# Where a two-layer decoder kernel reads the second copy of feature tile 0, and where it builds its bias table

## The chip, the cores and the metric

The kernel runs on one core of one Trainium2 chip. The metric is device time in microseconds (us), the median of several runs. The profile is one execution on the same kind of chip, recorded instruction by instruction.

## The reference

A batch of one sequence of 256 tokens with 1024 features passes through two layers, all in float32. Layer 0 has a gated short convolution and a gated feed-forward net (ConvGLU, 2816 hidden features). Layer 1 has block attention with 16 heads over keys and values computed once, and a second ConvGLU. Cut to what matters here:

```python
def rms_norm(x, g):
    y = x * lax.rsqrt(jnp.mean(x * x, axis=-1, keepdims=True) + EPS)
    return y * g
...
x = x + short_conv_mixer(rms_norm(x, a_norm), a_w_in, a_conv, a_w_out)   # layer 0
x = x + conv_glu_ffn(rms_norm(x, f_norm[0]), ...)
k, v, k_mean = shared_kv(x, kv_norm, w_k, w_v)
x = x + moba_attention(rms_norm(x, b_norm), w_q, w_o, k, v, k_mean, rel_bias)   # layer 1
x = x + conv_glu_ffn(rms_norm(x, f_norm[1]), ...)
return rms_norm(x, final_norm)
```

With 256 tokens there is a single attention block, so attention is plain causal softmax attention with a bias that depends on the distance between two tokens (`rel_bias`, 32 buckets by 16 heads).

## The kernel before, in words

**Products in three parts.** Activations are kept transposed, features on the 128 partitions and the 256 tokens along a row, as eight feature tiles k = 0 to 7. Every float32 weight block and every activation is split into a high and a low part, and a product is three TensorE matmuls (`mm3`, L163 to L166): high weights by high activations (`xh`, L164), high weights by low activations (`xl`, L165), low weights by high activations (L166). Nearly all of them load 128x128 weights and stream 256 columns. `up_step` (L168) runs a 1 MB unit of weights (two halves, 8 tiles, 3 matmuls: 48) or a 512 KB unit (24) into one PSUM bank; `down_step` (L194) is 24 matmuls into four banks. ScalarE makes the high parts (L86), VectorE the low ones (L92), SyncE (SP) issues the loads (L80), three units ahead.

**Norms come late.** The products run on activations that are scaled by the gain alone, and each result is multiplied by the root of its token afterwards. So each of the four stages with a norm (mixer, FFN of layer 0, V, FFN of layer 1) has two small products in true float32 in the middle of its first units, and both interrupt the stream of split matmuls. The first, in `rstd_cols` (L323), adds up the squares: "the sums of squares". VectorE then takes the root (L327, L308 to L313) and builds a diagonal matrix `dg` (L331). The second, in `rstd_rows` (L337), multiplies `ones` by `dg`: "the spread of the roots" over the partitions. The code places each by hand between two parts of an `up_step`, with the feature tiles left and right of it written out.

**The second copy.** `Rows` (L246) lays out `xh` and `xl`. The eight tiles start at element 48 + 256 of a row; a second place for tile 0, `again`, starts at element 32. With 4 bytes each, the eight tiles begin at byte 1216 = 9 x 128 + 64 of their row and `again` at byte 128 = 1 x 128: seen in steps of 128 bytes, the copy lies half a step off from the tiles. In the mixer and in layer 0's FFN, `tile_0_again` (L262) copies tile 0 there, and `up_step(..., again=True)` reads the copy in place of tile 0. In layer 1's FFN (`moved=True`) tile 0 lives only in that second place, so each of that FFN's 22 units reads it there, whatever `again` says.

In before, the copy is read in these places of layer 0: right behind the sums of squares of the mixer (L427) and of the FFN (L525); right behind the spread of the roots of the mixer (L435: tiles 0, 3 to 7, with 1 and 2 ahead of it) and of the FFN (L529, unit 2); and in unit 4 of the mixer (L459), right behind the bias table.

**The bias table.** `bias_table` (L346) is a third float32 product, `rb` by a one-hot matrix `hot`, 33 by 16 by 384. ScalarE copies it out of PSUM (L350) and stores it to DRAM (`ext_d`, L351), from where SP loads a piece per head pair (`bias_pair`, L353), the first one after V's unit 2. In before the product stands in the mixer, between its second `down_step` and unit 4 (L456), in the `misc` bank; `rb` and `hot` are loaded at the start (L153, L155).

Of the kernel before, what the change touches and what calls it, by code (L numbers as in the profile page):

```python
# [11 lines left out]
F32 = mybir.dt.float32  # L12
# [30 lines left out]
def yoco_kernel(ctx: ExitStack, tc: tile.TileContext, t: dict, out: bass.AP):  # L43
    nc = tc.nc
# [5 lines left out]
    tmp = ctx.enter_context(tc.tile_pool(name="tmp", bufs=2))  # L50
    dram = ctx.enter_context(tc.tile_pool(name="dram", bufs=1, space=bass.MemoryType.DRAM))
    psum = ctx.enter_context(tc.tile_pool(name="psum", bufs=1, space=bass.MemoryType.PSUM))
# [61 lines left out]
    MC = [Unit(t["w_mc"][j], BIG) for j in range(KT)]  # L114
# [35 lines left out]
        u.load()  # L150
    nc.sync.dma_start(pk[:, P_FCW:], t["pk"][:, P_FCW:])
    rb = tmp.tile([33, NH], F32, name="rb", bufs=1)
    nc.sync.dma_start(rb, t["rb"])  # L153
    hot = tmp.tile([33, 384], F32, name="hot", tag="sc", bufs=3)
    nc.sync.dma_start(hot, t["hot"])  # L155
    ident = const.tile([128, 128], F32, name="ident")
    make_identity(nc, ident)

# [9 lines left out]
    def up_step(u, o, xh, xl, m, ks=range(KT), first=0, again=False):  # L168

        assert u.lo is not None  # L170
        wh, wl = u.v(u.hi, m), u.v(u.lo, m)
        for k in ks:
            h, lw = (xh.again, xl.again) if again and k == 0 else (xh[:, k, :], xl[:, k, :])
            for i in range(m):
                mm3(o[:, i, :], wh[:, k, i, :], wl[:, k, i, :], h, lw,
                    start=(k == first and i == 0), stop=(k == KT - 1))
        u.used = ks[-1] == KT - 1
# [52 lines left out]
    def up_bank():  # L230
        return psum.tile([128, 2, S], F32, name="up", bufs=3)
# [111 lines left out]

    ext_d = dram.tile([NH, 384], F32, name="ext_d")

    def bias_table():  # L346
        ps = psum.tile([128, 512], F32, name="misc", bufs=1)
        PE.matmul(ps[:NH, :384], rb, hot, start=True, stop=True)
        e = tmp.tile([NH, 384], F32, name="ext", tag="pr", bufs=4)
        A.activation(e, ps[:NH, :384], AF.Copy)  # L350
        nc.scalar.dma_start(ext_d, e)  # L351
# [17 lines left out]
    mc, mb, z = {}, {}, {}  # L369
# [58 lines left out]
    mb[1] = acc_bank()  # L428
    up_step(MB[1], mb[1], xh, xl, 1)
    mc[2] = up_bank()  # L430
    up_step(MC[2], mc[2], xh, xl, 2, (1, 2), first=1)
    rr = rstd_rows(dg)
    A.activation(rr[:, 1, :], rr[:, 0, :], AF.Square)
    lo("S")
    up_step(MC[2], mc[2], xh, xl, 2, (0, 3, 4, 5, 6, 7), first=1, again=True)  # L435
    mb[2] = psum.tile([128, 512], F32, name="misc", bufs=1).rearrange("p (a s) -> p a s", s=S)
    up_step(MB[2], mb[2], xh, xl, 1)
    for i in range(2):
# [13 lines left out]
    for i in range(2):  # L452
        down_step(MO[i], acc, z[i], first=(i == 0))
        hi("S")
        lo("S")
    bias_table()  # L456
    for j in range(4, KT):
        mc[j] = up_bank()
        up_step(MC[j], mc[j], xh, xl, 2, again=(j == 4))  # L459
        o = mixer_a(j, "S")  # L460
        mb[j] = up_bank()
        up_step(MB[j], mb[j], xh, xl, 1)
        hi("S")
        mixer_b(j, o, "B" if j < KT - 1 else "S")
        if j < KT - 1:
            lo("S")
        if j == KT - 3:
            lo("B")
        down_step(MO[j - 2], acc, z[j - 2])
        hi("S")  # L470
        if j == KT - 1:
            lo("S")
# [8 lines left out]
    def ffn(layer, xh, xl, sq, bank=down_bank, between=None):  # L481
        ub, hd, low = {}, {}, {}
        up, dn = UP[layer], DN[layer]

        def conv(j, last=False):
            c0 = 2 * FJ * layer + j
            cw = [[par(P_FCW, 3 * (c0 + half * FJ) + n) for n in range(3)] for half in range(2)]
            u = tmp.tile([128, 2, S], F32, name="u", bufs=2)
            V.tensor_mul(u, ub[j], rr[:, 0:1, :].to_broadcast([128, 2, S]))  # L489
            if j:  # L490
                low[j - 1]()
            if not last:
                lo("B")
            o = tmp.tile([128, 2, S], F32, name="cv", bufs=2)
            for half in range(2):
                A.activation(o[:, half, :], u[:, half, :], AF.Identity, scale=cw[half][2],  # L496
                             bias=par(P_FCB, c0 + half * FJ))
            hi("B")
            for back in (1, 2):
                for half in range(2):  # L500
                    tap(o[:, half, :], u[:, half, :], cw[half][2 - back], back)
            return o

        def gate(j, o, last=False):
            sl = tmp.tile([128, S], F32, name="sl", tag="sc", bufs=3)
            hi("S")
            A.activation(sl, o[:, 0, :], AF.Silu)
            lo("S", 0, 1 + last)
            hid = tmp.tile([128, S], F32, name="hid", tag="pr", bufs=4)
            V.tensor_mul(hid, sl, o[:, 1, :])  # L510
            hd[j], zh, low[j] = split_act(hid, S)
            zh()
            if last:
                lo("S", 1, 2)
                low[j]()

        acc = None
        for i in range(FJ):
            ub[i] = up_bank()
            if i == 1:  # L520
                up_step(up[1], ub[1], xh, xl, 2, range(1, 4), first=1)
                _, dg = rstd_cols(sq)
                lo("S")
                A.activation(first, ones[:, 0:1], AF.Silu)
                up_step(up[1], ub[1], xh, xl, 2, (0, 4, 5, 6, 7), first=1, again=True)  # L525
                rr = rstd_rows(dg)
                gate(0, conv(0))
            else:
                up_step(up[i], ub[i], xh, xl, 2, again=(i == 2))  # L529
            last = i == FJ - 1  # L530
            if i:
                o = conv(i, last)
                if not last:
                    gate(i, o)
            if i == 0 and between:
                between()
            if i >= LAG:
                if i == LAG:
                    acc = [acc_bank() for _ in range(4)]
                down_step(dn[i - LAG], acc, hd[i - LAG], first=(i == LAG), bank=bank)  # L540
            if last:
                gate(i, o, True)
            elif i == FJ - 2:
                hi("S")
                lo("S")
            if i == 0:
                hi("B")
        if bank is token_bank:
            token_last(dn[FJ - 3:], acc, [hd[j] for j in range(FJ - 3, FJ)])
        else:  # L550
            down_step(dn[FJ - 3], acc, hd[FJ - 3])
            down_last(dn[FJ - 2:], acc, [hd[FJ - 2], hd[FJ - 1]])
        return acc

    acc = ffn(0, xh, xl, sq)


    xvh, xvl, sq = boundary(acc, xT, P_KVN, rev)
    xqh, xql = parts_tiles()
    vh = wpool.tile([128, 2, D], F32R, name="vh", tag="hiB2")  # L560
# [155 lines left out]
    for kind, n in heads:  # L716
        if kind == "v":
            vb[n] = acc_bank() if n < 3 else up_bank()
            if n == 1:
                v_step(1, range(0, 4))  # L720
                ycol, dg = rstd_cols(sq)
                v_step(1, range(4, 8))
                oh = shifted(act, "oh", "oh", KT, bufs=1)
            elif n == 2:
                v_step(2, range(0, 2))
                rr = rstd_rows(dg, (-0.125, 1.0), (rev, same))
                v_step(2, range(2, 8))
                bias[0] = bias_pair(0)
            else:
                v_step(n)  # L730
# [181 lines left out]
```

## Time and profile before

| | us |
|---|---|
| median of 3 runs | 594.75 (594.44 to 594.77) |
| the profiled execution's own time | 594.58 |
| its span in the trace | 592.5 |
| TensorE matmul (PE) busy | 583.1, 98%, 4745 records |
| weight load (PEld) busy | 568.1, 96% |
| VectorE (DVE) busy | 461.0, 78% |
| ScalarE (ACT) busy | 359.7, 61% |
| GpSimd (POOL) busy | 3.6, 1% |

The profiled execution took 2.1 us more than its span. A matmul's record starts when the matmul starts and ends when its last result is out, so the records overlap: 0.28 us long, they start every 0.11 to 0.12 us. How fast the stream runs is therefore read from the starts, over many matmuls, not from the busy share. In the rows of the timeline the columns are start, duration, engine, line, operation, tiles out<-in, shape and count.

### The profile page before, as it was taken

To read this page: it belongs to the slowest core of one execution; us is meant where nothing else is said; L and a number is where in the kernel's file an instruction comes from. 1 tells how busy PE (TensorE), PEld (TensorE's weight loads), DVE (VectorE), ACT (ScalarE), POOL (GpSimd) and SP (SyncE) were. 2 spreads that over 40 slices of the span, in tenths; PEclk is the share of its full clock that TensorE was granted. 3 is DMA by queue.
4 is the path that set the end of the run, shared out by engine and by line. 5 is a ranking of instruction groups with operands and counts; after the bars stand their busy time and mean duration, and the time that the engine had idled before them with its cause. 6 is when DMAs were issued, how large, how long until landed. Compare 5 with 4: busy or idle time off the path is not lost.

```text
span 592.5 us, 11536 instructions
## 1 busy us (share of the span) xinstructions
PE 583.1 (98%) x4745; PEld 568.1 (96%) x4745; DVE 461.0 (78%) x781; ACT 359.7 (61%) x570; POOL 3.6 (1%) x15
## 2 busy tenths in 40 slices
PE   8999999999999999999999999999999999999995
PEld 8999999999999999999999999999999999999994
DVE  5998769888877787778887898747997877778765
ACT  7765337566654565455767999738675655556434
POOL 0000000000000000000000000000000000000001
PEclk9999999999999999999999999999999999999998
DMA  8975583546445544554355564442646445553211
GB/s 294 401 282 180 177 285 109 176 144 248 159 168 210 212 156 170 210 208 149 108 189 221 197 210 157 170 142 106 241 152 238 177 165 202 213 203 117 72 37 71
DMA packets 24236, 108.51 MB, mean 183 GB/s; under 512 B 2759, under 2 KB 5496, under 8 KB 16248
## 3 DMA queue, kind: packets, MB, share of 16 engines
q1 hardware_dynamic: 23864, 107.46, 50.4%
q8 instruction: 37, 0.61, 0.4%
q10 hardware_dynamic: 320, 0.32, 0.2%
q14 instruction: 15, 0.12, 0.1%
HBM read 106.70 MB, written 1.07 MB: 182 GB/s over the span
## 4 chain that ended last, share of the span: by engine, by line
PE 97%; DMA 1%; ACT 1%; DVE 0%; issue 0%; SPq 0%; POOLq 0%; POOL 0%; DVEq 0%; ACTq 0%
PE up L164 20%; PE up L165 20%; PE up L166 20%; PE acc L164 7%; PE acc L165 7%; PE acc L166 7%; PE acc L192 3%; PE acc L191 3%; PE acc L190 3%; PE acc L619 1%; PE acc L575 1%; PE acc L578 1%; PE acc L577 1%; DMA xres<-xT 1%; PE up L578 0%; PE up L575 0%
## 5 line engine op out<-in xcount | busy, mean ns | idle before, releaser
L164 PE MATMUL up<-xh,hiB 128*128 128x256 f32 x944 | 265.6, 281 | 0.7 <-ACT hiB L86 0.6
L166 PE MATMUL up<-xh,loB 128*128 128x256 f32 x944 | 263.9, 280 | 0.5 <-DVE loB L92 0.5
L165 PE MATMUL up<-xl,hiB 128*128 128x256 f32 x944 | 264.0, 280 | 0.0
L164 PEld LDWEIGHTS up<-xh,hiB 128*128 128x128 f32 x944 | 179.5, 190 | 2.7 <-ACT hiB L86 1.1
L166 PEld LDWEIGHTS up<-xh,loB 128*128 128x128 f32 x944 | 177.4, 188 | 0.9 <-DVE loB L92 0.9
L165 PEld LDWEIGHTS up<-xl,hiB 128*128 128x128 f32 x944 | 177.3, 188 | 0.8
L92 DVE TENSOR_TENSOR loB<-rawB,hiB 128x2048 fp32r<-128x2048 f32 (+2 forms) x75 | 147.5, 1972 | 3.6 <-ACT hiB L86 3.5
L86 ACT ACTIVATE hiB<-rawB 128x2048 fp32r<-128x2048 f32 (+1 forms) x73 | 123.4, 1694 | 19.4 <-issue 6.2
L496 ACT ACTIVATE cv<-u,pk 128x256 f32<-128x256 f32 x88 | 48.2, 595 | 79.2 <-DVE u L489 79.2
L92 DVE TENSOR_TENSOR loS<-rawS,hiS 128x1024 fp32r<-128x1024 f32 (+2 forms) x73 | 83.6, 1146 | 14.4 <-ACT hiS L86 14.0
L366 DVE SCALAR_TENSOR_TENSOR cv<-u,pk,cv 128x255 f32<-128x255 f32 x192 | 81.2, 477 | 2.6 <-ACT cv L496 1.7
L489 DVE TENSOR_TENSOR u<-up,rr 128x512 f32<-128x512 f32 x44 | 30.3, 690 | 64.9 <-PE up L166 63.6
L86 ACT ACTIVATE hiS<-rawS 128x1024 fp32r<-128x1024 f32 (+1 forms) x71 | 71.6, 1010 | 11.8 <-PE acc L165 7.6
L166 PE MATMUL acc<-sh,loS 128*128 128x256 f32 x240 | 67.5, 281 | 0.0
L165 PE MATMUL acc<-sl,hiS 128*128 128x256 f32 x240 | 67.5, 281 | 0.0
L164 PE MATMUL acc<-sh,hiS 128*128 128x256 f32 x240 | 67.5, 281 | 0.0
L363 ACT ACTIVATE sh<-hid 128x256 fp32r<-128x256 f32 x52 | 21.7, 417 | 59.7 <-DVE hid L510 54.9
L164 PEld LDWEIGHTS acc<-sh,hiS 128*128 128x128 f32 x240 | 46.1, 192 | 0.0
L166 PEld LDWEIGHTS acc<-sh,loS 128*128 128x128 f32 x240 | 45.1, 188 | 0.0
L165 PEld LDWEIGHTS acc<-sl,hiS 128*128 128x128 f32 x240 | 45.1, 188 | 0.0
L192 PE MATMUL acc<-hiS,sl 128*128 128x512 f32 (+1 forms) x89 | 34.9, 392 | 0.0
L191 PE MATMUL acc<-loS,sh 128*128 128x512 f32 (+1 forms) x89 | 34.7, 390 | 0.0
(157 smaller groups left out, 757.2 us busy)
## 6 DMA issues: line engine op xcount, KB each, us to landing
rawB<-w_up SPq DMA_DIRECT2D x44, 1024.0 KB, 4.8
rawS<-w_dn SPq DMA_DIRECT2D x44, 512.0 KB, 3.4
rawB<-w_qk SPq DMA_DIRECT2D x8, 1024.0 KB, 4.8
rawB<-w_mc SPq DMA_DIRECT2D x6, 1024.0 KB, 8.8
rawS<-w_mo SPq DMA_DIRECT2D x8, 512.0 KB, 4.1
rawB<-w_v SPq DMA_DIRECT2D x4, 1024.0 KB, 4.7
rawS<-w_o SPq DMA_DIRECT2D x8, 512.0 KB, 3.4
rawS<-w_mb SPq DMA_DIRECT2D x7, 512.0 KB, 5.6
```

The lines of the kernel that those rows point to most:

```text
L86: A.activation(self.hi[:, c], self.raw[:, c], AF.Copy)
L92: V.tensor_sub(self.lo[:, c], self.raw[:, c], f32(self.hi[:, c]))
L164: PE.matmul(o, wh, xh, start=start, stop=False, skip_group_check=True)
L165: PE.matmul(o, wh, xl, start=False, stop=False, skip_group_check=True)
L166: PE.matmul(o, wl, xh, start=False, stop=stop, skip_group_check=True)
L190: PE.matmul(o, hh[:, tok], u.hi[:, f], start=first, stop=False, skip_group_check=True)
L191: PE.matmul(o, hh[:, tok], u.lo[:, f], start=False, stop=False, skip_group_check=True)
L192: PE.matmul(o, hl[:, tok], u.hi[:, f], start=False, stop=last, skip_group_check=True)
L363: return (h, lw), lambda: A.activation(h, src, AF.Copy), lambda: V.tensor_sub(lw, src, f32(h))
L366: V.scalar_tensor_tensor(o[:, back:], u[:, :S - back], w, o[:, back:], op0=OP.mult, op1=OP.add)
L489: V.tensor_mul(u, ub[j], rr[:, 0:1, :].to_broadcast([128, 2, S]))
L496: A.activation(o[:, half, :], u[:, half, :], AF.Identity, scale=cw[half][2], bias=par(P_FCB, c0 + half * FJ))
```

## The change

- Behind the spread of the roots, layer 0 reads tile 0 in its place among the eight: the mixer's unit 2 runs tiles 0 and 1 ahead of it and 2 to 7 behind it, and the FFN's unit 2 runs 0 to 7. Behind the sums of squares of the mixer and of layer 0's FFN the copy stays.
- In layer 1's FFN, unit 1 runs tiles 0 to 2 ahead of the sums of squares and 3 to 7 behind them (before: 1 to 3, then 0 and 4 to 7).
- The bias table's product moves from the mixer to V's stage, right ahead of the sums of squares there, and into a bank of the `up` pool. `rb` and `hot` are loaded after layer 0's FFN. The mixer's unit 4 no longer reads the copy.

```diff
     rb = tmp.tile([33, NH], F32, name="rb", bufs=1)
-    nc.sync.dma_start(rb, t["rb"])
-    hot = tmp.tile([33, 384], F32, name="hot", tag="sc", bufs=3)
-    nc.sync.dma_start(hot, t["hot"])
...
-    def bias_table():
-        ps = psum.tile([128, 512], F32, name="misc", bufs=1)
+    def bias_load():
+        nc.sync.dma_start(rb, t["rb"])
+        hot = tmp.tile([33, 384], F32, name="hot", tag="sc", bufs=3)
+        nc.sync.dma_start(hot, t["hot"])
+        return hot
+
+    def bias_table(hot):
+        ps = up_bank().rearrange("p a s -> p (a s)")
...
-    up_step(MC[2], mc[2], xh, xl, 2, (1, 2), first=1)
+    up_step(MC[2], mc[2], xh, xl, 2, range(0, 2))
     rr = rstd_rows(dg)
...
-    up_step(MC[2], mc[2], xh, xl, 2, (0, 3, 4, 5, 6, 7), first=1, again=True)
+    up_step(MC[2], mc[2], xh, xl, 2, range(2, 8))
...
-    bias_table()
     for j in range(4, KT):
         mc[j] = up_bank()
-        up_step(MC[j], mc[j], xh, xl, 2, again=(j == 4))
+        up_step(MC[j], mc[j], xh, xl, 2)
...
             if i == 1:
-                up_step(up[1], ub[1], xh, xl, 2, range(1, 4), first=1)
+                ks = ((1, 2, 3), (0, 4, 5, 6, 7)) if layer == 0 else (range(0, 3), range(3, 8))
+                up_step(up[1], ub[1], xh, xl, 2, ks[0], first=ks[0][0])
                 _, dg = rstd_cols(sq)
...
-                up_step(up[1], ub[1], xh, xl, 2, (0, 4, 5, 6, 7), first=1, again=True)
+                up_step(up[1], ub[1], xh, xl, 2, ks[1], first=ks[0][0], again=True)
...
-                up_step(up[i], ub[i], xh, xl, 2, again=(i == 2))
+                up_step(up[i], ub[i], xh, xl, 2)
...
+    hot = bias_load()
     xvh, xvl, sq = boundary(acc, xT, P_KVN, rev)
...
                 v_step(1, range(0, 4))
+                bias_table(hot)
                 ycol, dg = rstd_cols(sq)
```

The lines of the changed kernel are numbered 3 less than before's from L153 to L343 and then up to 5 more, so L164 is L161 and L323 is L320 there.

The number of matmuls and their order by weights stay the same in the mixer but for the bias table; which copy of tile 0 a row reads is not in its name (`xh` stands for both). On TensorE before, between the last rows of the mixer's second `down_step` (`acc<-sh`) and the first of unit 4 (`up<-xh`):

```order
L164 MATMUL acc<-sh,hiS_516 128x256
L165 MATMUL acc<-sl,hiS_516 128x256
L166 MATMUL acc<-sh,loS_574 128x256
L348 MATMUL misc<-hot,rb 16x384
L164 MATMUL up<-xh,hiB_469 128x256
L165 MATMUL up<-xl,hiB_469 128x256
```

In the changed kernel the same place is without it, and from the spread of the roots to FFN 0's sums of squares no float32 product is left:

```order
L161 MATMUL acc<-sh,hiS_513 128x256
L162 MATMUL acc<-sl,hiS_513 128x256
L163 MATMUL acc<-sh,loS_571 128x256
L161 MATMUL up<-xh,hiB_466 128x256
L162 MATMUL up<-xl,hiB_466 128x256
L163 MATMUL up<-xh,loB_494 128x256
```

The float32 product has left this place; the rows around it are the same.

On TensorE of the changed kernel in the middle of V's unit 1, whose rows read `acc<-hiB,xh` because the weights stream there and the activations are loaded:

```order
L579 MATMUL acc<-hiB_3340,xh 128x256
L581 MATMUL acc<-loB_3590,xh 128x256
L582 MATMUL acc<-hiB_3340,xl 128x256
L351 MATMUL up<-hot,rb 16x384
L320 MATMUL misc<-ones,sq 128x1 x2
L579 MATMUL acc<-hiB_3340,xh 128x256
```

The table now stands right against the sums of squares, in a bank of its own. On SP's queue, around the loads of the first attention weights (`w_o`, `w_qk`), as a piece of the difference:

```order
 L80 DMA rawB<-w_qk 128x2048
 L80 DMA rawS<-w_o 128x1024 x3
+L344 DMA rb<-rb 33x16
+L346 DMA hot<-hot 33x384
 L80 DMA rawB<-w_qk 128x2048 x3
-L355 DMA bias<-ext_d 128x2x256
+L358 DMA bias<-ext_d 128x2x256
 L80 DMA rawB<-w_qk 128x2048 x2
```

The two small loads moved there from the start of the program; the first piece of the bias is still asked for behind the same three weight loads.

## The prediction

> **What bounds the kernel now.** The first view is the page's chain of work that ended last:
>
> ```profile
> PE 97%; DMA 1%; ACT 1%; DVE 0%; issue 0%; SPq 0%; POOLq 0%; POOL 0%; DVEq 0%; ACTq 0%
> ```
>
> 97% of it is TensorE running matmuls, not waiting for them. So the time is the number of matmuls times the step from one start to the next, and the question is whether that step is the same everywhere. The busy times by stretch (per stretch: length, PE, PEld, DVE, ACT, POOL busy, granted clock, DMA share, GB/s) exclude the clock:
>
> ```profile
> 30.00:46.00 16.00, 16.00 (x138) 16.00 (x138) 15.03 (x26) 9.67 (x13) 0.00 (x0) 1.00 0.69 251
> 120.00:280.00 160.00, 160.00 (x1361) 160.00 (x1360) 122.69 (x184) 90.05 (x120) 0.00 (x0) 1.00 0.51 185
> 392.73:400.85 8.12, 8.12 (x74) 8.12 (x73) 4.40 (x8) 2.88 (x5) 0.00 (x0) 1.00 0.33 116
> ```
>
> The granted clock is 1.00 in the FFN of layer 0 (second row) and in the attention's output product (third). Then I took starts from the timeline of TensorE, same shape of matmul in both stretches:
>
> ```profile
> 125.11 0.28 PE L164 MATMUL up<-xh,hiB 128*128 128x256 f32 x1
> ...
> 274.92 0.28 PE L164 MATMUL acc<-sh,hiS 128*128 128x256 f32 x1
> ...
> 395.45 0.28 PE L164 MATMUL acc<-oh,hiS 128*128 128x256 f32 x1
> ...
> 400.89 0.28 PE L164 MATMUL up<-xh,hiB 128*128 128x256 f32 x1
> ```
>
> From 125.11 to 274.92 the FFN starts 18 up units and 17 down units, 18 x 48 + 17 x 24 = 1272 matmuls: 149.81 / 1272 = 117.8 ns a step. From 395.45 to 400.89 two output units start 48: 5.44 / 48 = 113.3 ns. Same shape, same clock, nobody waiting, and yet two tempos that differ by 4.45 ns. I call them slow and fast.
>
> Last I followed the tempo over the two small float32 products of a norm, here in the mixer:
>
> ```profile
> 19.46 0.50 PE L323 MATMUL misc<-ones,sq 128*128 128x1 f32 x4
> ...
> 20.02 0.28 PE L165 MATMUL acc<-xl,hiB 128*128 128x256 f32 x1
> ...
> 20.61 0.28 PE L164 MATMUL acc<-xh,hiB 128*128 128x256 f32 x1
> ...
> 21.30 0.28 PE L164 MATMUL acc<-xh,hiS 128*128 128x256 f32 x1
> ...
> 25.26 0.28 PE L166 MATMUL up<-xh,loB 128*128 128x256 f32 x1
> 25.38 0.59 PE L337 MATMUL misc<-dg,ones 128*128 128x256 f32 x2
> 25.62 0.47 PE L164 MATMUL up<-xh,hiB 128*128 128x256 f32 x1
> 25.93 0.28 PE L165 MATMUL up<-xl,hiB 128*128 128x256 f32 x1
> ...
> 26.53 0.28 PE L164 MATMUL up<-xh,hiB 128*128 128x256 f32 x1
> ...
> 70.58 0.28 PE L164 MATMUL up<-xh,hiB 128*128 128x256 f32 x1
> ...
> 79.06 0.28 PE L164 MATMUL acc<-sh,hiS 128*128 128x256 f32 x1
> ```
>
> Behind the sums of squares (19.46) the copy of tile 0 runs first, six matmuls: 118 ns a step (20.02 to 20.61, five steps). Then come the tiles in their places, and the stream is fast: 35 steps from 21.30 to 25.26, 113.1 ns. Behind the spread of the roots (25.38) the copy also runs first, at 120 ns (25.93 to 26.53), but here the stream stays slow: 8.48 / 72 = 117.8 ns from 70.58 to 79.06. The FFN of layer 0 is slow from 125.11 on, behind its own spread at 110.53, and layer 1's does the same:
>
> ```profile
> 110.53 0.59 PE L337 MATMUL misc<-dg,ones 128*128 128x256 f32 x2
> ...
> 414.07 0.59 PE L337 MATMUL misc<-dg,ones 128*128 128x256 f32 x2
> ...
> 415.21 0.28 PE L164 MATMUL up<-xh,hiB 128*128 128x256 f32 x1
> ...
> 420.16 0.28 PE L164 MATMUL up<-xh,hiB 128*128 128x256 f32 x1
> ```
>
> (42 steps from 415.21, 117.9 ns.) So the copy behind the spread went with a slow stream three times out of three.
>
> **Spread of the roots: tile 0 in its place.** This is the term that decides, and no row shows it: nowhere in before does `up_step` go on behind the spread without the copy. The nearest rows are the plain tiles behind other interruptions:
>
> ```profile
> 332.81 0.28 PE L164 MATMUL up<-xh,hiB 128*128 128x256 f32 x1
> ...
> 335.19 0.28 PE L164 MATMUL up<-xh,hiB 128*128 128x256 f32 x1
> ...
> 408.48 0.28 PE L164 MATMUL up<-xh,hiB 128*128 128x256 f32 x1
> ...
> 408.82 0.28 PE L164 MATMUL up<-xh,hiB 128*128 128x256 f32 x1
> ...
> 316.52 0.28 PE L165 MATMUL up<-xl,hiB 128*128 128x256 f32 x1
> ...
> 317.11 0.28 PE L164 MATMUL up<-xh,hiB 128*128 128x256 f32 x1
> ```
>
> Right behind the products with V (332.81, 21 steps: 113.3 ns) and right behind sixteen float32 transposes (408.48, 3 steps: 113 ns) plain tiles are fast within a few matmuls. Behind the attention's scores (316.52, 5 steps: 118 ns) they stay slow; that stream was slow already. The changed places are entered fast (21.30 to 25.26 above), like 408.48, so I take the fast end as likelier. If plain tiles land fast, it pays until the next float32 product:
>
> - Mixer, now without the bias table, up to FFN 0's sums of squares: 36 + 24 (unit 2 and its gate), 48 + 24, 48 (two down units), 4 x 96, 48 (last two), then 48 + 18 in the FFN: 678 matmuls x 4.45 ns = 3.0 us.
> - FFN of layer 0: 20 up units and 22 down units, 20 x 48 + 22 x 24 = 1488 x 4.45 ns = 6.6 us.
>
> Against it stand some ten matmuls of settling at each of the two, 0.1 us. If they land slow, both terms are 0. A tempo slower than 117.8 ns that lasts shows nowhere in these rows, so the spread's term has no loss below that.
>
> What hides the other engines then? In layer 0's FFN VectorE is busy 122.7 of 160 us, so a stream 4% faster leaves it room. In the mixer at 30 to 46 us it is busy 15.03 of 16: if it became the end there, the gain of that stretch would be lost, 138 x 4.45 ns = 0.6 us. That is my bound on the weak side; I take none of it, since TensorE waited for nothing there.
>
> The Trainium skill, "SBUF — State Buffer", section "Who interferes with whom", says that "PE and ACT never wait on anyone", which would leave no room for where a tile lies. "TensorE: Matmul & The Clock Gate", section "Back-to-back issue gap", gives a warm step of N / 2.4 + 2.5 ns, so an estimate of 109.2 ns for 256 columns wherever they lie; by these two the two terms would be 0 and the sum that of the bias table alone. The trace has 113.3 and 117.8 ns at granted clock 1.00, so neither tempo is that figure, and one shape has two.
>
> **Bias table.** Its price in the mixer:
>
> ```profile
> 46.90 0.28 PE L166 MATMUL acc<-sh,loS 128*128 128x256 f32 x1
> 47.11 0.81 PE L348 MATMUL misc<-hot,rb 33*16 33x384 f32 x2
> 47.86 0.39 PE L164 MATMUL up<-xh,hiB 128*128 128x256 f32 x1
> 48.08 0.28 PE L165 MATMUL up<-xl,hiB 128*128 128x256 f32 x1
> ```
>
> From 46.90 to 48.08 run two ordinary matmuls (0.24 us) and the table: 0.94 us. In V's stage it costs the same at most, and less by the way into float32 and back, which the sums of squares next to it pay anyway: 47.11 - 46.90 - 0.12 = 0.09 and 48.08 - 47.86 - 0.12 = 0.10 us. So the move brings 0 to 0.2 us; I take 0.1. The rest hides:
>
> ```profile
> 293.91 0.89 ACT L268 ACTIVATE xh<-xres,pk 128x256 fp32r<-128x256 f32 x2
> 298.18 1.92 ACT L86 ACTIVATE hiB<-rawB 128x2048 fp32r<-128x2048 f32 x1 [3.38 <-PE acc L578]
> ```
>
> ```profile
> 291.60 11.41 SPq L80 DMA_DIRECT2D rawB<-w_qk  x3
> 303.07 0.43 SPq L355 DMA_DIRECT2D bias<-ext_d  x1
> ```
>
> ```profile
> ext_d<-ext ACTq DMA_DIRECT2D x1, 24.0 KB, 3.4
> ```
>
> ScalarE idles 3.38 us here, and there the copy out of PSUM and its store are queued. From 294.8 on and with 3.4 us to landing the table is in DRAM at about 299, an estimate from these rows; SP asks for its first piece at 303.07, behind the three weight loads. That is 4 us of cover; beyond it SP would wait, and the `w_qk` loads queued behind, and TensorE with them, would come late microsecond for microsecond. The two small loads stand on SP ahead of the three weight loads; the bank and the buffer that table and `hot` take were last used three units before the end of FFN 0.
>
> **Layer 1's unit 1.** Tile 3 instead of the moved tile 0 runs behind the sums of squares. Bounds: 30 matmuls to the spread, all slow, 30 x 4.45 ns = 0.13 us lost; or, if that puts the spread's stream right, the two units up to the first down unit, 96 x 4.45 = 0.43 us won. Behind the spread itself tile 0 is still read from its moved place, as in the slow rows from 414.07, so I take 0.1 us lost.
>
> **The sum**, on the profiled execution's 594.58 us: -3.0 - 6.6 + 0.1 - 0.1 + 0.1 = -9.5, so 585.1. The median of the runs is 0.17 higher than that execution: 585.25, say 585.2. Its own range: 0.6 us weaker for VectorE and 0.1 + 0.1 more for bias and unit 1, up to 586.3; stronger by 0.5 for unit 1 and 0.1 for the bias, down to 584.6.
>
> **The rivals.**
>
> 1. *Plain tiles land slow behind the spread too.* For it: 316.52, and the spread's 0.59 us is a longer interruption than the sums' 0.50. Against it: the other plain rows. The time: 594.75 - 0.1 + 0.1 = 594.75. Chance 0.18.
> 2. *Where tile 0 lies does nothing; the product before sets the tempo,* sums fast, spread slow. For it: three spreads of three with a slow stream behind them. Against it: in the mixer the six matmuls on the copy run at 118 to 120 ns and the tiles in place right behind the first six at 113.1, so the place does change a step. It gives the same 594.75, at most 594.9. Chance 0.11. By the Trainium skill's sentence quoted above this would be the outcome.
> 3. *Only one of the two stages turns fast,* because the mixer goes on with tile 2 and the FFN with tile 0: FFN alone 594.75 - 6.6 = 588.15, mixer alone 591.75. Against it: each tile is 1024 bytes, so all begin alike. Chance 0.06.
> 4. *Slower: the attention's fast stretch goes slow.* It begins at 332.81 and ends at 400.89; four query units (4 x 48) and the output units (8 x 24) in it are 384 matmuls. The table, a float32 product of 33 rows put into V's stage, shifts the stream that attention starts from; if that tips every re-entry, 384 x 4.45 ns = 1.7 us is lost, and with rival 1 that makes 596.45. It decides from 270 of the 384 on. Against it: the stream came into attention slow as it is and turned fast only at 332.81, four units behind the place. Chance 0.05.
>
> **How the numbers follow.** The forecast has 0.60. Faster or slower means over 0.2%, 1.2 us, about what a measurement can tell from no change. Faster: forecast and rival 3, 0.66. Same: rivals 1 and 2, 0.29. Slower: 0.05. The forecast and rival 3 hold only 0.66, so the range reaches on to rivals 1 and 2: from 584.6, less 0.2 for what the starts' rounding leaves open in 4.45 ns, to 594.9: 584.4 to 594.9.
>
> **What would show it.** In the changed profile, starts behind the mixer's and FFN 0's spread should be 113.3 ns apart within some ten matmuls and stay so: 72 steps of the mixer in 8.16 us, not 8.48. The span should shrink by 3 us up to FFN 0's sums of squares (plus 0.94 for the table) and by 6.6 us from there to V. Attention should keep its tempo by place. The forecast is wrong if steps of 117.8 ns follow either spread, or if the fast stream meets waits of TensorE for VectorE in the mixer.

## The result, and the profile after

The changed kernel takes 584.26 us (median of 4 runs, 584.08 to 584.58), before 594.74 us beside it (median of 4, 594.44 to 594.77). The ratio is 0.9825 with the interval 0.9808 to 0.9842: 10.5 us faster. The forecast was 585.2, with a stated range of 584.4 to 594.9. The two large terms came as forecast, but the time lies 0.14 us below the range: the gain is 0.9 us larger than the sum had it, and the sum left a term out. Which one is worked out behind the experiments.

The profiled execution took 584.08 us, its span is 582.1 us, 10.4 shorter than before's. The page's busy times and the chain that ended last, after:

```profile
PE 573.4 (98%) x4745; PEld 558.4 (96%) x4745; DVE 460.9 (79%) x781; ACT 359.7 (62%) x570; POOL 3.6 (1%) x15
...
PE 97%; DMA 1%; ACT 1%; DVE 0%; issue 0%; SPq 0%; POOLq 0%; POOL 0%; DVEq 0%; ACTq 0%
```

Same 4745 matmul records, same 97% of the chain, but 9.7 us less of PE: nothing stopped waiting, the matmuls came closer together. All tempos below are read from starts; where a matmul's record ends is used nowhere, and no run shows that it is when the last result is out. The busy times by stretch (length, PE, PEld, DVE, ACT, POOL, granted clock, DMA share, GB/s), after:

```profile
30.00:46.00 16.00, 16.00 (x144) 16.00 (x143) 15.03 (x26) 9.68 (x13) 0.00 (x0) 1.00 0.73 250
120.00:264.00 144.00, 144.00 (x1273) 144.00 (x1272) 113.89 (x166) 86.11 (x113) 0.00 (x0) 1.00 0.54 193
```

The clock is 1.00 as before. In the 16 us of the mixer 144 matmul records start where 138 did, and in the FFN of layer 0 the 1272 steps that took 149.81 us take 144.16 (120.58 to 264.74 in the rows below), 113.3 ns each. VectorE, busy 15.03 of 16 us in the mixer, did not become the end there: from 27.05 us to the FFN's sums of squares 666 steps take 75.48 us, 113.3 ns each.

To see where the 10.4 us lie, I divided both traces at the same instructions. TensorE's timeline, after, at the mixer's spread, layer 0's sums of squares, the 1272 steps of its FFN, the start of V, and in V the last matmul ahead of the float32 products, the table, the second matmul behind the sums, and the spread:

```profile
25.34 0.59 PE L334 MATMUL misc<-dg,ones 128*128 128x256 f32 x2
...
102.64 0.50 PE L320 MATMUL misc<-ones,sq 128*128 128x1 f32 x4
...
120.58 0.28 PE L161 MATMUL up<-xh,hiB 128*128 128x256 f32 x1
...
264.74 0.28 PE L161 MATMUL acc<-sh,hiS 128*128 128x256 f32 x1
...
275.62 0.28 PE L579 MATMUL acc<-hiB,xh 128*128 128x256 f32 x1
...
283.67 0.28 PE L582 MATMUL acc<-hiB,xl 128*128 128x256 f32 x1
283.88 0.81 PE L351 MATMUL up<-hot,rb 33*16 33x384 f32 x2
...
285.29 0.28 PE L581 MATMUL acc<-loB,xh 128*128 128x256 f32 x1
...
289.26 0.59 PE L334 MATMUL misc<-dg,ones 128*128 128x256 f32 x2
```

The same instructions in before's timeline, as far as the prediction has not shown them (where a view ends inside a row, here and in later views, its duration and its count are smaller than in a wider view; its start is the same):

```profile
106.62 0.50 PE L323 MATMUL misc<-ones,sq 128*128 128x1 f32 x4
...
286.23 0.28 PE L575 MATMUL acc<-hiB,xh 128*128 128x256 f32 x1
...
294.60 0.28 PE L578 MATMUL acc<-hiB,xl 128*128 128x256 f32 x1
...
295.27 0.28 PE L577 MATMUL acc<-loB,xh 128*128 128x256 f32 x1
...
299.40 0.38 PE L337 MATMUL misc<-dg,ones 128*128 128x256 f32 x1
...
410.19 0.50 PE L323 MATMUL misc<-ones,sq 128*128 128x1 f32 x4
...
430.38 0.28 PE L164 MATMUL up<-xh,hiB 128*128 128x256 f32 x1
```

And layer 1's FFN after, from its sums of squares over its spread into its first units:

```profile
400.10 0.50 PE L320 MATMUL misc<-ones,sq 128*128 128x1 f32 x4
...
400.66 0.28 PE L162 MATMUL up<-xl,hiB 128*128 128x256 f32 x1
...
403.96 0.28 PE L163 MATMUL up<-xh,loB 128*128 128x256 f32 x1
404.08 0.60 PE L334 MATMUL misc<-dg,ones 128*128 128x256 f32 x2
...
405.92 0.28 PE L161 MATMUL up<-xh,hiB 128*128 128x256 f32 x1
...
410.00 0.28 PE L161 MATMUL up<-xh,hiB 128*128 128x256 f32 x1
...
419.99 0.28 PE L161 MATMUL up<-xh,hiB 128*128 128x256 f32 x1
```

The difference of the starts gives the account:

| stretch | before, us | after, us | shorter by |
|---|---|---|---|
| mixer's spread to layer 0's sums | 106.62 - 25.38 = 81.24 | 102.64 - 25.34 = 77.30 | 3.94, of it 0.94 the table |
| on to V's first matmul | 286.23 - 106.62 = 179.61 | 275.62 - 102.64 = 172.98 | 6.63 |
| on to V's spread | 299.40 - 286.23 = 13.17 | 289.26 - 275.62 = 13.64 | -0.47 |
| on to layer 1's sums | 410.19 - 299.40 = 110.79 | 400.10 - 289.26 = 110.84 | -0.05 |
| on to an up unit behind layer 1's first down step | 430.38 - 410.19 = 20.19 | 419.99 - 400.10 = 19.89 | 0.30 |

Behind that the two run alike. The rows sum to 10.35, and 0.04 comes from the start. The third row has two parts. The table is in it now: from the last matmul ahead of the float32 products to the second one behind them it is 285.29 - 283.67 = 1.62 us against 295.27 - 294.60 = 0.67, so the table costs 0.95. The other part is a gain of 0.95 - 0.47 = 0.48: V's matmuls ahead of the products step 8.05 / 71 = 113.4 ns (before 8.37 / 71 = 117.9), and behind them 3.97 / 35 = 113.4 (before 4.13 / 35 = 118.0).

In layer 1's FFN plain tiles behind the sums now land slow, 28 steps in 3.30 us or 117.9 ns, and behind the spread the moved tile 0 lands fast, 36 steps from 405.92 in 4.08 us or 113.3 ns. Both are the other way round from before.

The bias table's way to DRAM, after: its store on ScalarE's queue, and SP's first request for a piece of it:

```profile
285.24 0.33 ACTq L354 DMA_DIRECT2D ext_d<-ext  x1
```

```profile
292.80 0.39 SPq L358 DMA_DIRECT2D bias<-ext_d  x1
```

The store is issued by 285.6 and lands 1.5 us later (the time from issue to landing of this one transfer in the list of DMA groups), so the table lies in DRAM 5.7 us before SP asks for it.

### The profile page after: what moved, and what is told of

It is laid out like the page before. It is cut to its first block, busy times and chain, and to the rows that moved or that the text cites. A ratio compares the mean times of both kernels' runs of the same rounds, so it can differ in the third digit from the quotient of the medians.

```text
span 582.1 us, 11537 instructions
## 1 busy us (share of the span) xinstructions
PE 573.4 (98%) x4745; PEld 558.4 (96%) x4745; DVE 460.9 (79%) x781; ACT 359.7 (62%) x570; POOL 3.6 (1%) x15
## 4 chain that ended last, share of the span: by engine, by line
PE 97%; DMA 1%; ACT 1%; DVE 0%; issue 0%; SPq 0%; POOLq 0%; POOL 0%; DVEq 0%; ACTq 0%
PE up L161 20%; PE up L163 20%; PE up L162 20%; PE acc L161 7%; PE acc L163 7%; PE acc L162 6%; PE acc L189 3%; PE acc L188 3%; PE acc L187 3%; PE acc L623 1%; PE acc L579 1%; PE acc L581 1%; PE acc L582 1%; DMA xres<-xT 1%; PE up L582 0%; PE up L579 0%
## 5 line engine op out<-in xcount | busy, mean ns | idle before, releaser
L161 PE MATMUL up<-xh,hiB 128*128 128x256 f32 x944 | 263.2, 279 | 0.3 <-ACT hiB L86 0.3
L161 PEld LDWEIGHTS up<-xh,hiB 128*128 128x128 f32 x944 | 177.5, 188 | 1.6 <-ACT hiB L86 0.6
L161 PE MATMUL acc<-sh,hiS 128*128 128x256 f32 x240 | 66.3, 276 | 0.0
L163 PE MATMUL acc<-sh,loS 128*128 128x256 f32 x240 | 66.3, 276 | 0.0
L162 PE MATMUL acc<-sl,hiS 128*128 128x256 f32 x240 | 66.3, 276 | 0.0
L161 PEld LDWEIGHTS acc<-sh,hiS 128*128 128x128 f32 x240 | 45.1, 188 | 0.0
```

What stands on the lines that cost most here:

```text
L161: PE.matmul(o, wh, xh, start=start, stop=False, skip_group_check=True)
L162: PE.matmul(o, wh, xl, start=False, stop=False, skip_group_check=True)
L163: PE.matmul(o, wl, xh, start=False, stop=stop, skip_group_check=True)
```

## The experiments

The theory after the result: a small float32 product lets the stream of split matmuls fall into one of two tempos, and which one is set by the phase of the reads right behind it, that is, by where within a 128-byte step they begin, and by the tempo with which the stream came in. Three rivals: it is the order of the feature tiles (the mixer now goes on with tile 2 and not with 0); it is the second copy as such, another place in memory, whatever its phase; part of the gain comes from the table's leaving the mixer. The step of 128 bytes is a yardstick and not a result: the places that are tried lie 0, 16, 32 or 64 bytes off the tiles' alignment, and apart from that whole multiples of 1024 bytes from a tile, so no run tells a step of 128 bytes from one of 256, 512 or 1024. Each edit is one on the changed kernel. m_copy, m_order, f_copy and table_mixer ran beside before at 594.70 us, f_entry, f_phase, best and swap beside 594.36, l1_copy, f_off16 and f_off32 beside 594.81.

**The mixer with order and copy as before (m_copy).**

```diff
-    up_step(MC[2], mc[2], xh, xl, 2, range(0, 2))
+    up_step(MC[2], mc[2], xh, xl, 2, (1, 2), first=1)
...
-    up_step(MC[2], mc[2], xh, xl, 2, range(2, 8))
+    up_step(MC[2], mc[2], xh, xl, 2, (0, 3, 4, 5, 6, 7), first=1, again=True)
```

> The changed kernel, with the mixer's unit 2 alone as it was before: tiles 1 and 2, the spread of the roots, then the copy of tile 0 and tiles 3 to 7. Theory 'place' (behind the spread the tempo is set by where the first six matmuls read; entered fast, the copy lands slow and a tile in its place lands fast): slow, 117.8 ns a step, from the mixer's spread to FFN 0's sums of squares, 678 x 4.45 ns = 3.0 us more: 587.3 us; layer 0's FFN stays at 113.3 ns. Rival 'table' (what turned the mixer fast is that the bias table left it): 584.3 us. Rival 'order' (which tiles stand left and right of the spread): 587.3 as well; m_order parts it.

Measured 587.19 us, ratio to before 0.9875 (0.9858 to 0.9891). TensorE's timeline of this kernel, from the mixer's spread to layer 0's sums, with 72 steps between:

```profile
24.92 0.59 PE L334 MATMUL misc<-dg,ones 128*128 128x256 f32 x2
...
69.18 0.28 PE L161 MATMUL up<-xh,hiB 128*128 128x256 f32 x1
...
77.66 0.28 PE L161 MATMUL acc<-sh,hiS 128*128 128x256 f32 x1
...
105.22 0.39 PE L320 MATMUL misc<-ones,sq 128*128 128x1 f32 x3
```

The stretch takes 80.30 us, 3.00 more than after's 77.30, and the 72 steps 8.48 / 72 = 117.8 ns. The FFN behind it is as fast as in the changed kernel.

**The same order, without the copy (m_order).**

```diff
-    up_step(MC[2], mc[2], xh, xl, 2, range(0, 2))
+    up_step(MC[2], mc[2], xh, xl, 2, (1, 2), first=1)
...
-    up_step(MC[2], mc[2], xh, xl, 2, range(2, 8))
+    up_step(MC[2], mc[2], xh, xl, 2, (0, 3, 4, 5, 6, 7), first=1)
```

> The changed kernel, with the mixer's unit 2 in before's order of tiles (1, 2, spread, 0, 3 to 7), but tile 0 read in its place and not from the copy. Theory 'place': 584.3 us, 113.3 ns a step behind the spread. Rival 'order': 587.3 us, 117.8 ns behind the spread. Rival 'table': 584.3 us.

Measured 584.46 us, ratio 0.9827 (0.9812 to 0.9842). Spread and sums in its timeline:

```profile
25.07 0.38 PE L334 MATMUL misc<-dg,ones 128*128 128x256 f32 x1
...
102.37 0.16 PE L320 MATMUL misc<-ones,sq 128*128 128x1 f32 x1
```

From spread to sums it takes 77.30 us, the changed kernel's figure to the hundredth. So the order does nothing here; the rival of the order falls, and the 3.0 us are those of the copy.

**Layer 0's FFN with the copy in unit 2 (f_copy).**

```diff
-                up_step(up[i], ub[i], xh, xl, 2)
+                up_step(up[i], ub[i], xh, xl, 2, again=(i == 2 and layer == 0))
```

> The changed kernel, with the copy of tile 0 behind the spread of layer 0's FFN alone (unit 2, as before). Theory 'place': 117.8 ns a step through that FFN, 1488 x 4.45 ns = 6.6 us, and through V's units 0 and half of 1, which then come in slow again, 108 x 4.45 ns = 0.5 us: 591.4 us; the mixer stays at 113.3 ns. Rival 'table': 584.3 us, since the table is out of the mixer.

Measured 591.27 us, ratio 0.9944 (0.9929 to 0.9959). Its timeline at layer 0's sums, the 1272 steps and V's start:

```profile
102.82 0.39 PE L320 MATMUL misc<-ones,sq 128*128 128x1 f32 x3
...
121.28 0.28 PE L161 MATMUL up<-xh,hiB 128*128 128x256 f32 x1
...
271.09 0.28 PE L161 MATMUL acc<-sh,hiS 128*128 128x256 f32 x1
...
282.40 0.28 PE L579 MATMUL acc<-hiB,xh 128*128 128x256 f32 x1
```

149.81 / 1272 = 117.8 ns, before's tempo to the hundredth of a microsecond, and 179.58 us from the sums to V against 172.98: 6.60 us for six matmuls that read the same numbers from another place. The slow stream runs on to the next float32 products: V's first 71 steps take 8.36 us here, 0.31 more than after. Behind the table and the sums V is fast again, though it came in slow: 34 steps from 292.39 in 3.85 us, 113.2 ns. The expectation had counted these as slow too.

**The copy in a third place, at the tiles' phase (f_phase).** As f_copy, but unit 2 reads a third copy of tile 0, which starts at element 48 + 9 x 256 of the row: byte 9408 = 73 x 128 + 64, the phase of the eight tiles. (The expectation calls this 2048 bytes behind the tiles' first. It is 2048 elements, so 8192 bytes or 64 steps of 128; the phase is the same.)

```diff
-            h, lw = (xh.again, xl.again) if again and k == 0 else (xh[:, k, :], xl[:, k, :])
+            h, lw = (xh.again, xl.again) if again is True and k == 0 else (xh.third, xl.third) if again and k == 0 else (xh[:, k, :], xl[:, k, :])
...
-            t = act.tile([128, (KT + 1) * S + 64], F32R, name=name, tag=name)
+            t = act.tile([128, (KT + 2) * S + 64], F32R, name=name, tag=name)
+            self.third = t[:, 48 + (KT + 1) * S:48 + (KT + 2) * S]
...
+        A.activation(xh.third, f32(xh[:, 0, :]), AF.Copy)
+        V.tensor_copy(xl.third, f32(xl[:, 0, :]))
...
-                up_step(up[i], ub[i], xh, xl, 2)
+                up_step(up[i], ub[i], xh, xl, 2, again=(i == 2 and layer == 0) * 3)
```

> As f_copy, but unit 2 of layer 0's FFN reads tile 0 from a third place, 2048 bytes (16 steps of 128) behind the eight tiles' first, so at the same point of a 128-byte step as the tiles. Behind the sums of squares the copy half a step off stays. Theory 'phase' (what counts is where in a 128-byte step the read begins): lands fast like a tile in its place, 584.3 us. Rival 'second tile' (any jump to another buffer for tile 0): as f_copy, 591.3 us.

Measured 583.90 us, ratio 0.9825 (0.9812 to 0.9839). Sums and V's start in its timeline:

```profile
102.68 0.28 PE L323 MATMUL misc<-ones,sq 128*128 128x1 f32 x2
...
275.66 0.28 PE L582 MATMUL acc<-hiB,xh 128*128 128x256 f32 x1
```

172.98 us, the same as with plain tiles. A copy is harmless behind the spread if its phase is that of the tiles, and the rival of the copy as such falls.

**The third place 16 and 32 bytes further (f_off16, f_off32).** As f_phase, but for one line each:

```diff
+            self.third = t[:, 52 + (KT + 1) * S:52 + (KT + 2) * S]
```

```diff
+            self.third = t[:, 56 + (KT + 1) * S:56 + (KT + 2) * S]
```

> As f_phase (tile 0 from a third place behind the spread of layer 0's FFN), but 16 bytes further, an eighth of the 128-byte step. It asks how fine the phase is. Theory 'half steps count' (the read's 64-byte half of the step decides, 16 bytes stay inside it): fast, 584 us. Theory 'any offset counts': slow through FFN 0 and V's first units, 591 us.

> As f_phase, but 32 bytes further, a quarter of the 128-byte step, half way to the copy's phase. Theory 'half steps count': the read begins inside the same 64 bytes but its lines are crossed half way; I expect fast, 584 us, with less confidence than at 16 bytes. Theory 'any offset counts': slow, 591 us.

Sums and V's start in the timelines of f_off16 (the first two rows) and f_off32:

```profile
102.18 0.28 PE L323 MATMUL misc<-ones,sq 128*128 128x1 f32 x2
...
275.18 0.28 PE L582 MATMUL acc<-hiB,xh 128*128 128x256 f32 x1
```

```profile
102.21 0.28 PE L323 MATMUL misc<-ones,sq 128*128 128x1 f32 x2
...
281.78 0.28 PE L582 MATMUL acc<-hiB,xh 128*128 128x256 f32 x1
```

f_off16: 583.79 us (2 runs), ratio 0.9817 (0.9797 to 0.9836), 173.00 us from the sums to V: fast. f_off32: 590.88 us (2 runs), ratio 0.9936 (0.9916 to 0.9956), 179.57 us: slow, where I had leant towards fast. An eighth of the step off lands fast; a quarter, like the half of f_copy, lands slow. Sixteen bytes of one buffer part the two, so the distance to the tiles and the buffer are not the cause. The phase decides, by a rule that these points don't give.

**Entering layer 0's spread slow (f_entry).** As f_copy, and the sums of layer 0's FFN are followed by plain tiles, as in layer 1 of the changed kernel.

```diff
-                ks = ((1, 2, 3), (0, 4, 5, 6, 7)) if layer == 0 else (range(0, 3), range(3, 8))
+                ks = (range(0, 3), range(3, 8))
...
-                up_step(up[i], ub[i], xh, xl, 2)
+                up_step(up[i], ub[i], xh, xl, 2, again=(i == 2 and layer == 0))
```

> As f_copy (copy of tile 0 behind the spread of layer 0's FFN), but behind that FFN's sums of squares the tiles run in plain order (0 to 2, sums, 3 to 7), as in layer 1 of the changed kernel, where the copy landed fast behind a spread that was entered slow. Theory 'place and entry' (where the stream lands depends on its tempo before the product as well as on the place): the sums land slow, the spread is entered slow and the copy behind it lands fast: 0.1 us over the changed kernel, 584.4 us. Theory 'place alone' (the copy behind a spread is slow whatever comes before): as f_copy, 591.3 us.

Measured 583.96 us, ratio 0.9825 (0.9812 to 0.9839). Its timeline from the second matmul behind the sums to the spread, and behind it:

```profile
103.01 0.28 PE L162 MATMUL up<-xl,hiB 128*128 128x256 f32 x1
...
106.31 0.28 PE L163 MATMUL up<-xh,loB 128*128 128x256 f32 x1
106.43 0.60 PE L334 MATMUL misc<-dg,ones 128*128 128x256 f32 x2
...
107.94 0.28 PE L161 MATMUL up<-xh,hiB 128*128 128x256 f32 x1
...
112.02 0.28 PE L161 MATMUL up<-xh,hiB 128*128 128x256 f32 x1
```

Behind the sums 28 steps take 3.30 us, 117.9 ns, so the spread is entered slow. Behind it the very copy that cost f_copy 6.60 us lands fast: 36 steps in 4.08 us, 113.3 ns. From the sums to V it is 173.11 us, 0.13 more than after, the price of the slow unit. So the copy is not bad behind the spread as such: the tempo turns over there, from fast to slow in f_copy, from slow to fast here. That the entry decides is the reading that fits all runs, but it isn't shown alone: every slow entry comes with another order of tiles in unit 1, and no run enters a spread slow and goes on with a tile in its place. Behind the sums of squares the entry does not matter in the runs: the copy lands fast there whether the stream came in fast (after) or slow (before at 106.62, m_copy at 105.22; in both the last 17 steps up to the spread take 1.93 us, 113.5 ns).

**Layer 1's sums as before (l1_copy).**

```diff
-                ks = ((1, 2, 3), (0, 4, 5, 6, 7)) if layer == 0 else (range(0, 3), range(3, 8))
+                ks = ((1, 2, 3), (0, 4, 5, 6, 7))
```

> The changed kernel with layer 1's unit 1 in before's order (tiles 1 to 3, sums of squares, moved tile 0, 4 to 7); unit 2 still begins with the moved tile 0 behind the spread. It prices the layer-1 edit alone. Theory 'place and entry': the copy lands fast behind the sums, the spread is entered fast and the moved tile lands slow behind it, as in before: in the trace 0.25 us more between that FFN's sums and its first down unit's end, 584.5 us. Theory 'place alone': 0.1 us less than the changed kernel, since the spread's landing would be the same in both.

Measured 584.13 us, ratio 0.9824 (0.9808 to 0.9841); a few tenths are not to be had from medians, since the way to the mixer's sums of squares alone takes 18.89 us (best) to 19.60 us (f_copy) in the profiled executions. The trace tells it: behind layer 1's sums, and from its spread to the same matmul as 419.99 after:

```profile
400.28 0.28 PE L162 MATMUL up<-xl,hiB 128*128 128x256 f32 x1
...
403.48 0.28 PE L163 MATMUL up<-xh,loB 128*128 128x256 f32 x1
403.60 0.59 PE L334 MATMUL misc<-dg,ones 128*128 128x256 f32 x2
...
419.91 0.28 PE L161 MATMUL up<-xh,hiB 128*128 128x256 f32 x1
```

With the moved tile behind the sums, 28 steps take 3.20 us instead of 3.30, and the spread is entered fast. Then the moved tile lands slow: 16.31 us from the spread on (before: 430.38 - 414.07, also 16.31) against after's 15.91. So the edit in unit 1 loses 0.10 us behind the sums and wins 0.40 behind the spread.

**The table back in the mixer (table_mixer).** The two loads at the start, the product ahead of unit 4 in the `misc` bank as in before, but unit 4 with plain tiles.

```diff
+    bias_table(hot)
     for j in range(4, KT):
...
-                bias_table(hot)
```

> The changed kernel, with the bias table back in the mixer and its loads at the start, unit 4 plain. It prices the move alone. Theory 'place' does not say how plain tiles land behind this product of 33 rows: if fast, 0.94 us for the table in the mixer against 0.7 in V, 584.5 us; if slow, 498 x 4.45 ns = 2.2 us more, 586.7 us, with FFN 0 fast again behind its own sums of squares. Rival 'table' (the gain is its leaving the mixer): 587 us or more, slow from the table to the end of the mixer and on through FFN 0 (594 us).

Measured 583.73 us, ratio 0.9815 (0.9800 to 0.9829). In the mixer the table costs 0.96 us, and plain tiles behind it land fast. Its timeline in V, behind the sums up to the spread, and behind the spread from V's last matmuls over the first query units:

```profile
285.12 0.28 PE L578 MATMUL acc<-loB,xh 128*128 128x256 f32 x1
...
289.12 0.28 PE L579 MATMUL acc<-hiB,xl 128*128 128x256 f32 x1
...
293.44 0.28 PE L579 MATMUL acc<-hiB,xl 128*128 128x256 f32 x1
...
304.35 0.28 PE L166 MATMUL up<-xh,loB 128*128 128x256 f32 x1
```

Without the table ahead of them, V's sums land slow: 4.00 us / 34 = 117.6 ns (after: 113.4). But the two query units then run at 10.91 / 96 = 113.6 ns; in the changed kernel the same 96 steps take 11.30 us, 117.7 ns. Up to the end of the query products this kernel wins 0.58 us there and loses 0.16 at the sums, 0.42 in all. The span is 581.5 against 582.1, of which 0.19 is the start. So the table's move gained nothing: its own price is the same in both places, and the tempo that the stream has in V and attention behind it costs 0.4 us. These tenths are read from one trace of each kernel, and the move is that of the product, its bank and its loads together. And the tempo changes here without a float32 product: V's last 23 steps take 2.71 us (291.08 to 293.79), 117.8 ns, and the query units behind them run at 113.6, so that the border where the streaming operand changes from weights to activations can turn it too; in the changed kernel the tempo stays slow there.

**The phases exchanged (swap).** The copy now starts at byte 64 of the row, the eight tiles at byte 1152 = 9 x 128.

```diff
-            self.again = t[:, 32:32 + S]
-            self.rows = t[:, 48 + S:48 + S + KT * S].rearrange("p (k s) -> p k s", s=S)
+            self.again = t[:, 16:16 + S]
+            self.rows = t[:, 32 + S:32 + S + KT * S].rearrange("p (k s) -> p k s", s=S)
```

> The changed kernel with the two phases exchanged: the eight tiles begin at a full 128-byte step of their row and the copy half a step off; nothing else moves. Theory 'phase': a 113.3 ns tempo exists only for the tiles' present phase against the weights; the copy's own six matmuls took 118 to 119 ns in fast streams too. Then all up and query units run at 118 to 119 ns, some 2600 matmuls that are fast in the changed kernel x 5 ns = 13 us: 597 us (592 to 601, by whether the down units, whose operands do not move, keep their tempo). Rival 'no phase' (the copy's matmuls are slow only from the jump): about 584 us.

Measured 599.01 us, ratio 1.0082 (1.0068 to 1.0095): slower than before, and about 15 us slower than the changed kernel (spans 597.1 and 582.1). 72 `up` matmuls of the mixer in its timeline:

```profile
33.12 0.28 PE L161 MATMUL up<-xh,hiB 128*128 128x256 f32 x1
...
41.66 0.28 PE L161 MATMUL acc<-sh,hiS 128*128 128x256 f32 x1
```

8.54 / 72 = 118.6 ns at a granted clock of 1.00, a third tempo that neither kernel has. The up and query units keep it throughout, in a pattern of six steps of some 114 to 122 ns; the down units, whose activations lie elsewhere, run at 113 or 118. So the phase is not only a matter of landing: with the tiles at the other phase the fast tempo of the up units is gone.

**What the runs suggested (best).** As table_mixer, and in layer 1 the sums as in l1_copy and the moved tile as the seventh in unit 2 rather than the first, so that plain tiles follow its spread.

```diff
-                up_step(up[i], ub[i], xh, xl, 2)
+                l1 = layer == 1 and i == 2
+                up_step(up[i], ub[i], xh, xl, 2, (1, 2, 3, 4, 5, 6, 0, 7) if l1 else range(KT), first=int(l1))
```

> The kernel with the table back in the mixer (583.7 us), and in layer 1's FFN the copy behind the sums of squares (tiles 1 to 3, sums, moved tile 0, 4 to 7) and unit 2 with tile 0 next to last, so that a tile in its usual phase comes first behind the spread. Theory 'place and entry': both land fast there, about 24 matmuls x 4.45 ns = 0.1 us less: 583.6 us. Theory 'place alone' says the same for the spread. If the spread lands slow, 90 matmuls x 4.45 ns = 0.4 us more, 584.1 us.

Measured 583.33 us (median of 5), ratio 0.9819 (0.9805 to 0.9832). Layer 1's stream lands fast behind both its sums and its spread. It beats before by 11 us; its interval overlaps that of the changed kernel, so that it beats that one too is read from the trace alone (span 581.1 against 582.1, of which 0.45 is the start and 0.42 the table's place, as in table_mixer).

## Why the prediction was right in its mechanism, and which step of its sum failed

- **The step that failed is the list under "it pays until the next float32 product".** The rule was right, but the list ended at FFN 0's 22 down units, and so put V at nothing, without a reason. The next float32 products are in V's unit 1, 72 matmuls on: their 71 steps take 8.05 us in place of 8.37, 0.32 less, which f_copy loses again (0.31). Another 36 behind V's sums went fast as well, 0.16 us; table_mixer, where they are slow, shows that they owe it to the table ahead of the sums. Together 0.48 us were missing, and no allowance of the range stood for them. With them the range, other things as stated, would have begun at 583.9, and 584.26 would lie inside.
- **Two tempos, and the copy behind the spread sets the slow one:** right for layer 0, and now shown by m_copy beside m_order and by f_copy, each with one cause. Plain tiles land fast behind both spreads. Mixer 3.0 forecast, 3.00 measured (3.94 with the table); FFN of layer 0 6.6 forecast, 6.63 measured. The 0.1 us that I set against them for settling does not show.
- **Layer 1's unit 1, "behind the spread itself tile 0 is still read from its moved place, as in the slow rows from 414.07, so I take 0.1 us lost":** this term had the wrong sign. I took the moved place itself for the cause of the slow stream; with the slow entry that the edit made, the same place lands fast. The slow unit behind the sums that I had priced at 0.13 us lost is there (0.10, and 0.05 ahead of the sums), and the spread's stream turns fast, worth 0.40: net 0.25 won in place of 0.1 lost. I had treated the two bounds as alternatives; both came true. The range had 0.5 us for this one.
- **Bias table, 0.1 won:** failed in size. It costs 0.95 us in V and 0.94 in the mixer; standing next to the sums saves it nothing. Its cover held with 5.7 us where I had estimated 4.
- **The sum:** 9.5 forecast, + 0.1 for no settling, + 0.48 for V, + 0.35 for layer 1, - 0.1 for the table makes 10.3, against 10.4 in the span. All of the shortfall lies in terms that I took as small, and three of the four lay on one side and added up. Had they cancelled, the time would have come into the range by luck, with the term for V missing all the same. The range's weak side was also added up wrongly: 585.2 + 0.6 + 0.2 is 586.0, not 586.3.
- **The rivals.** Plain tiles landing slow (1) fell at both spreads, though the thing exists: behind layer 1's sums they do. "The product sets the tempo" (2) fell by m_copy against m_order. It had more for it than the three spreads that were counted: V's spread in before, behind which no copy is read, goes with a slow stream as well (301.01 to 303.95, 25 steps of 117.6 ns). Only one stage (3) fell: both turned. Attention going slow (4) did not come: from V's spread to layer 1's sums the two kernels differ by 0.05 us, and that is unit 1's reading of tile 0 (l1_copy, which reads it as before does, has before's 110.79). Its idea, that the table shifts the stream that attention starts from, has something: table_mixer's query units are 0.58 us faster. Only, before did not have that gain either.
- The Trainium skill's sentence "PE and ACT never wait on anyone" ("SBUF — State Buffer", "Who interferes with whom") was cited as speaking for no effect. It speaks of one engine waiting for another and says nothing of where an operand lies, so it did not bear on the two terms. f_copy against f_phase, 6.9 us of TensorE's time in FFN and V for the phase of one tile, shows that TensorE's tempo does depend on that. Whether another engine has a part in it no run here shows.

**Open:** why a phase lands fast or slow, why the tempo then mostly stays until the next small product, and whether it is the tempo at entry or the order in unit 1 that turns the spread's landing over. V's spread lands slow whether it is entered fast (after) or slow (before); there the weights are what streams. And what sends table_mixer's query units fast, where before's, entered through a V of equal steps behind its sums, were slow, is not known.

## What to carry to other kernels

When TensorE is busy all the time and the clock is full, divide a long stretch of starts by its count, stage by stage: a few per cent between stages of one shape are a gain that no wait and no busy share shows. If such a tempo changes at an interruption, try what the first matmuls behind it read and at which offset, and look at all interruptions downstream, since an edit at one changes how the stream comes into the next. Count such a gain to the next interruption that really exists on the engine, and not to the end of the stage: here that was the term that the sum lacked.

## What the runs showed of the hardware

- The same matmul (128x128 weights, 256 columns, granted clock 1.00) stepped at 113.3, 117.8 or 118.6 ns. The Trainium skill, "TensorE: Matmul & The Clock Gate", "Back-to-back issue gap", gives N / 2.4 + 2.5 ns as the warm gap of an isolated matmul, from which the prediction's estimate of 109.2 ns is worked out. No stretch here reached it. The prediction took it for the step of a stream; the same section says that in a stream of weight loads and matmuls, which is what runs here, both set the spacing.
- The tempo has a memory. Six matmuls behind a 0.6 us interruption set it for more than 1500 that follow (f_copy, 6.6 us in the FFN and 0.3 in V), and what a given read does goes with the tempo at entry: behind the spread with the fast entry, the tiles' own phase stayed fast (after, f_phase) and half a step off turned slow (m_copy, f_copy, l1_copy); with the slow entry, half a step off turned fast (after's layer 1, f_entry). Behind the sums of mixer and FFN the copy landed fast, whatever the entry, and plain tiles slow (f_entry, layer 1 after). That it is the entry that counts behind the spread is argued, not shown alone.
- Offsets from the tiles' phase behind the spread, fast entry: 0 fast, 16 bytes fast, 32 bytes slow, 64 bytes slow.
- Exchanging the phases of tiles and copy, a move of both by 64 bytes in the layout and nothing else, cost about 15 us of 584.
